# Gate and up tiles of an FFN made by seven products instead of eight

## The chip, the cores and the metric

The kernel runs on one NeuronCore of a Trainium2 chip. The time of a run is its device time in microseconds. A profile describes one execution of the program; its span runs from the first to the last instruction.

Engines are named as in the profile: PE is TensorE's matmuls and PEld its weight loads, DVE is VectorE, ACT is ScalarE, POOL is GpSimd, SP issues most transfers.

## The reference

One inference step of a two-layer decoder trunk. 512 prompt tokens and 8 sample tokens stand side by side as 520 columns of an activation with 1024 features. Each layer is an FFN, a mixer (retention, windowed attention and a convolution over one input projection), and a second FFN:

```
x += 0.5 * (silu(h @ wg) * (h @ wu)) @ wd      h = rmsnorm(x), 1024 -> 2816 -> 1024
x += mix(rmsnorm(x))
x += 0.5 * (silu(h @ wg) * (h @ wu)) @ wd      the second FFN, weights of its own
```

Everything is in 32-bit floating point.

## The kernel before, in words

**Precision.** A 32-bit value is split into a high and a low part: ACT casts it to fp32r (`wh`, `xh`), DVE subtracts (`wl`, `xl`). A product is three matmuls: high by low, high by high, low by high. The activation is transposed, features on partitions and 520 columns along a row, and a matmul covers half of them (260 columns, `HN`). A tile of weights is 128 x 128. `mm3` (L320 to L326) issues the six matmuls of one weight tile; all of its matmuls carry L323.

**Weights.** They come as chunks of 128 x 1024 in the order of use, on SP's queue, into four raw buffers. `split_hi` (ACT, L272) and `split_lo` (DVE, L278) split them ahead of use. A chunk counts two slots, a product's weights (128 x 512) one, and `ahead` keeps everything within six slots of the current unit split.

**An FFN.** It has 22 hidden tiles of 128 features. `hidden` (L391) makes one: eight weight tiles for gate and eight for up, 96 matmuls, into two PSUM tiles. Then DVE multiplies gate by the norm's factor R (L399), ACT takes Silu (L401), DVE multiplies up by R (L402) and both together (L403): u, the hidden tile. Because R is multiplied in afterwards, xh and xl hold x times the norm's gain.

The order is fixed by `ffn_steps`: hidden 0 to 8, down 0, hidden 9 to 16, down 1, hidden 17 to 21, down 2. Down 0 and 1 take eight hidden tiles each in the 2x2 scheme; down 2 takes the last six by plain `mm3`.

**The 2x2 scheme** multiplies a 2 x 2 block matrix of weights by one of activations with seven block products instead of eight, at the price of sums of blocks. Here the blocks of activations are two feature tiles by two halves of the columns. `pair_blocks` (L406) makes them from two hidden tiles: four DVE subtractions (L411 to L414) and their splits (L336, L337). The sums of weights are DVE's too (`sums`, L240 to L245). `pair_down` (L426) runs the products a11, s1, s2, a12, s3, s4, a22 (`PRODUCTS`), each 12 matmuls (L315), and adds four result blocks into x (L433). Partial results are shared by copies on ACT: the first product's c11 is copied into c22 (L436), on which the third product s2 accumulates; two more copies (L439, L442) follow later. Three PSUM tiles of four are in use in one such sequence.

Before an FFN's down step, u of tile 8 (even, first of a pair) is only kept. u of tile 16 is split at once, by the two operations L336 and L337, because the last group isn't paired.

**Order of the engines.** The program is under a manual schedule: each engine runs its instructions in the order in which the Python code issues them.

**Buffers.** `units` is a pool of 20 buffers of 128 x 1040 values for blocks, splits and the mixer's tiles. `cc` holds all constants of the shapes, 2184 columns, loaded once at the start.

Of the kernel before, what the change touches and what calls it, by code (L numbers as in the profile page):

```python
# [10 lines left out]
F32 = mybir.dt.float32  # L11
F32R = mybir.dt.float32r
# [32 lines left out]

C_OFF, C_COLS = {}, 0
for _n, _w in (
    ("ident", 128), ("decT", 512), ("qdec", 256), ("kdec", 4), ("cd", 2), ("gs", 2),
    ("bias", 1024), ("bias32", 128), ("blk64", 128),
):  # L50
    C_OFF[_n] = C_COLS
    C_COLS += _w


def shape_constants():
# [77 lines left out]
def step_kernel(ctx: ExitStack, tc: tile.TileContext, io: dict):  # L133
    nc = tc.nc

    def pool(name, bufs, **kw):
        return ctx.enter_context(tc.tile_pool(name=name, bufs=bufs, **kw))
# [1 line left out]
    const = pool("const", 1)  # L139
    wraw = pool("wraw", RAW)  # L140
    wspl = pool("wspl", 3)
    units = pool("units", 20)
    work = pool("work", 6)
    small = pool("small", 1)
    psum = pool("psum", 4, space=bass.MemoryType.PSUM)
# [7 lines left out]

    Rd = const.tile([128, 2, NT], F32, name="Rd")
    par = const.tile([128, DEPTH, P_COLS], F32, name="par")
    cc = const.tile([128, C_COLS], F32, name="cc")
    epst = const.tile([128, 1], F32, name="epst")
    ones = {}

    def cst(name, *shape):  # L160
        n = int(np.prod(shape))
        a = cc[:, C_OFF[name] : C_OFF[name] + n]
        if len(shape) == 2:
            a = a.rearrange("p (a b) -> p a b", a=shape[0])
        return a
# [38 lines left out]
    for _ in range(DEPTH):  # L204
        for part in range(3):
            if part == 1:
                add_chunks(MIX_CHUNKS)
                continue
            for step, n in ffn_steps():
                if step == "hidden":  # L210
                    add_chunks(2 * KD // CT)
                elif GROUPS[n][2]:
                    add_products(KD // 2)
                else:
                    add_chunks((GROUPS[n][1] - GROUPS[n][0]) * KD // CT)
# [88 lines left out]
    def product(name, o, blocks, first):  # L304

        u, c = at
        assert seq[u][0] == name and c == 0
        ahead(u)
        at[0] = u + 1
        h, lo = spl[u]  # L310
        for j in range(JP):
            s = slice(j * 128, (j + 1) * 128)
            bh, bl = blocks[j][name]
            for i, (a, b) in enumerate(((h, bl), (h, bh), (lo, bh))):
                nc.tensor.matmul(  # L315
                    o, lhsT=a[:, s], rhs=b, start=first and j == 0 and i == 0, stop=j == JP - 1 and i == 2,
                    skip_group_check=True,
                )
# [16 lines left out]
    def split(h, lo, src):  # L335
        nc.scalar.copy(h, src)  # L336
        nc.vector.tensor_sub(lo, src, h.bitcast(F32))  # L337
# [41 lines left out]
    def norm():  # L379
        ah, al = wt("ah", dt=F32R), wt("al", dt=F32R)  # L380
        nc.scalar.copy(ah, acc)
        yield
        nc.vector.tensor_sub(al, acc, ah.bitcast(F32))
        yield
        o = ptile()
        colsum(o, ones[1024], (ah, al))
        yield
        yield from rsqrt(R, o)
        yield
# [13 lines left out]
        nc.vector.tensor_mul(u, u, t)  # L403
        return u

    def pair_blocks(u, w):  # L406


        (b11, b12), (b21, b22) = ((z[:, :HN], z[:, HN:]) for z in (u, w))
        p, q = wt("tp"), wt("tq")  # L410
        nc.vector.tensor_sub(p[:, :HN], b12, b11)  # L411
        nc.vector.tensor_sub(q[:, :HN], b12, b22)
        nc.vector.tensor_sub(p[:, HN:], b11, q[:, :HN])
        nc.vector.tensor_sub(q[:, HN:], b21, p[:, HN:])  # L414
        (bh, th), (bl, tl) = ((unit(F32R), unit(F32R)) for _ in range(2))
        for h, lo, c, n, src in (
            (bh, bl, 0, HN, b11), (bh, bl, HN, NT, w), (th, tl, 0, NT, p), (th, tl, NT, NT, q),
        ):
            split(h[:, c : c + n], lo[:, c : c + n], src[:, :n])
        at = dict(a11=(0, 0), a12=(0, 1), s4=(0, 2), s1=(1, 0), s2=(1, 1), s3=(1, 2), a22=(1, 3))  # L420
        return {
            name: tuple(z[i][:, c * HN : (c + 1) * HN] for z in ((bh, th), (bl, tl)))
            for name, (i, c) in at.items()
        }

    def pair_down(m, blocks):  # L426

        one, mid, c22 = ptile(), ptile(), ptile()[:, 0, :HN]
        c11, c21, m5, c12 = (t[:, i, :HN] for t in (one, mid) for i in range(2))

        def add(half, src, i=0, n=2):
            d = x[:, m + i : m + i + n, half * HN : (half + 1) * HN]
            nc.vector.scalar_tensor_tensor(d, src, 0.5, d, op0=ALU.mult, op1=ALU.add)  # L433

        product("a11", c11, blocks, True)
        nc.scalar.copy(c22, c11)  # L436
# [5 lines left out]
        nc.scalar.copy(c21, c22)  # L442
        product("s4", c12, blocks, False)
        add(1, c22.unsqueeze(1), 1, 1)
        add(1, c12.unsqueeze(1), 0, 1)
        add(1, m5.unsqueeze(1).to_broadcast([128, 2, HN]))
        product("a22", c21, blocks, False)
        add(0, one[:, :, :HN])

    def ffn(norm, after):  # L450
        hs, even = {n: [] for n in range(len(GROUPS))}, None
        for step, n in ffn_steps():
            if step == "hidden":
                g = next(i for i, (a, b, _) in enumerate(GROUPS) if a <= n < b)
                u = hidden(norm, n == 0)
                if not GROUPS[g][2]:
                    h = v2(unit(F32R))
                    hs[g].append((h[:, 0], h[:, 1]))
                    split(*hs[g][-1], u)
                elif n % 2:  # L460
                    hs[g].append(pair_blocks(even, u))
                else:
                    even = u
                continue
            if GROUPS[n][2]:
                for m in range(0, KD, 2):
                    pair_down(m, hs[n])
                continue
            for m in range(KD):
                o = ptile()  # L470
                for f, h in enumerate(hs[n]):
                    mm3(o, next_tile(), *h, f == 0, f == len(hs[n]) - 1)
                nc.vector.scalar_tensor_tensor(
                    v2(x[:, m]), o[:, :, :HN], 0.5, v2(x[:, m]), op0=ALU.mult, op1=ALU.add
                )
                if n == len(GROUPS) - 1:
                    run(after(m))

    def mix(l, after):
# [394 lines left out]
        def ret_vs():  # L874
            o = ptile()
            nc.tensor.transpose(o[:32, 0, :128], vs.rearrange("p h b -> p (h b)"), ident)
            yield
            vst = small.tile([32, 128], F32, tag="vst", name="vst")
            nc.scalar.copy(vst, o[:32, 0, :128])
            sc = ret["sc"] = dram.tile([32, 128], F32, tag="sc", name="sc")  # L880
            nc.gpsimd.dma_start(sc, vst)
            yield
# [279 lines left out]
        yield  # L1162

    for l in range(DEPTH):
        ffn(norm() if l else first_norm, lambda m: prep(l, "mix_norm", m))
        mix(l, lambda m: prep(l, "ffn2_norm", m))
        if l + 1 < DEPTH:
            ffn(norm(), lambda m: prep(l + 1, "ffn1_norm", m))
        else:
            ffn(norm(), store)  # L1170


def host_arrays(i):
# [67 lines left out]
    a["cc"] = shape_constants()  # L1241
# [49 lines left out]
```

## Time and profile before

| | us |
|---|---|
| median of 3 runs | 1939.46 |
| lowest and highest of them | 1937.09, 1940.21 |
| profiled execution | 1931.96 |
| its span | 1930.2 |
| PE, DVE, ACT busy in the span | 1900.1, 1240.2, 789.8 |
| matmuls | 15806 |

The profiled execution's own time is 7.5 us under the median; sums made from its rows are set against its own time. In a row of a timeline the columns are the start, the duration, engine, line, operation, output<-inputs, shapes and count; in square brackets stands how long the engine had been idle and what released it. In a row of groups the columns after the bar are busy time in us and mean ns of one instruction. In a row of windows they are the stretch, its length, the busy time of PE, PEld, DVE, ACT and POOL with instruction counts, the granted TensorE clock (1.00 is full), the DMA share and GB/s.

### The profile page before, as it was taken

Reading aid. Unit: us, or ns where it says so; the run is one execution under the profiler, and the core shown is the slowest. Engines: PE = TensorE matmul, PEld = TensorE weight load, DVE = VectorE, ACT = ScalarE, POOL = GpSimd, SP = SyncE. Lnnn points to the kernel's source line nnn. Section 1 sums busy time; section 2 is a strip of 40 time slices with the busy share of each in tenths; the row PEclk is TensorE's granted clock in tenths of the full one; section 3 lists DMA queues with packets and bytes.
Section 4 is the critical chain, followed back from the end, with each engine's and each line's share of the span. In section 5 each row is a group of like instructions: output and inputs, shape, how many; then the busy total and the mean of one; then the engine's idle time right before and its main releaser. Section 6 shows DMA issues by size and latency. Waiting matters only on the chain.

```text
span 1930.2 us, 36738 instructions
## 1 busy us (share of the span) xinstructions
PE 1900.1 (98%) x15806; PEld 1884.4 (98%) x15806; DVE 1240.2 (64%) x1887; ACT 789.8 (41%) x1280; POOL 21.4 (1%) x48
## 2 busy tenths in 40 slices
PE   8999999999999999999999999999998999999999
PEld 8999999999889999999999999999998999999999
DVE  6585584688757575584555855746887565855843
ACT  5343342433764343343343433425338543433421
POOL 0000000000100000000000000000000000000000
PEclk9999999999999999999999999999999999999999
DMA  5223233333312323323222232323333132232321
GB/s 210 90 77 110 88 99 99 115 107 113 115 45 86 100 70 118 99 70 117 92 95 88 88 110 67 121 97 118 99 112 103 44 99 95 82 110 88 98 100 67
DMA packets 53588, 188.28 MB, mean 98 GB/s; under 512 B 6209, under 2 KB 6961, under 8 KB 53297
## 3 DMA queue, kind: packets, MB, share of 16 engines
q1 hardware_dynamic: 50784, 178.40, 28.2%
q0 software_dynamic: 2496, 7.43, 1.2%
q8 instruction: 124, 2.03, 0.4%
q14 instruction: 40, 0.32, 0.1%
q10 hardware_dynamic: 144, 0.11, 0.0%
HBM read 178.45 MB, written 7.45 MB: 96 GB/s over the span
## 4 chain that ended last, share of the span: by engine, by line
PE 95%; DVE 2%; ACT 2%; issue 0%; DMA 0%; POOL 0%; ACTq 0%; DVEq 0%
PE o L323 76%; PE o L315 16%; PE o L342 1%; DVE nt L360 0%; PE o L1004 0%; PE o L507 0%; PE o L768 0%; PE o L756 0%; DMA m<-sc 0%; PE o L956 0%; DVE rr L361 0%; ACT rsq L1017 0%; ACT m L741 0%; ACT y L357 0%; ACT m L993 0%
## 5 line engine op out<-in xcount | busy, mean ns | idle before, releaser
L323 PE MATMUL o<-xl,wh 128*128 128x260 f32 x3584 | 723.8, 283 | 6.7 <-DVE xl L368 5.8
L323 PE MATMUL o<-xh,wl 128*128 128x260 f32 x3584 | 722.8, 283 | 0.3 <-DVE wl L278 0.3
L323 PE MATMUL o<-xh,wh 128*128 128x260 f32 x3584 | 721.8, 283 | 0.0
L323 PEld LDWEIGHTS o<-xl,wh 128*128 128x128 f32 x3584 | 553.4, 189 | 7.7 <-ACT wh L336 5.8
L323 PEld LDWEIGHTS o<-xh,wl 128*128 128x128 f32 x3584 | 553.3, 189 | 0.5 <-DVE wl L278 0.5
L323 PEld LDWEIGHTS o<-xh,wh 128*128 128x128 f32 x3584 | 551.8, 188 | 0.0
L272 ACT CAST wh<-w 128x1024 fp32r<-128x1024 f32 (+1 forms) x318 | 306.3, 965 | 424.0 <-PE o L323 310.9
L278 DVE TENSOR_TENSOR wl<-w,wh 128x1024 fp32r<-128x1024 f32 x254 | 310.1, 1223 | 222.9 <-ACT wh L272 221.4
L402 DVE TENSOR_TENSOR u<-o,R 128x520 f32<-128x520 f32 x88 | 61.6, 700 | 231.3 <-PE o L323 231.3
L315 PE MATMUL o<-m,wh 128*128 128x260 f32 x1344 | 180.5, 283 | 8.1 <-ACT o L436 8.1
L315 PE MATMUL o<-m,wl 128*128 128x260 f32 x1344 | 179.6, 283 | 0.0
L315 PEld LDWEIGHTS o<-m,wh 128*128 128x128 f32 x1344 | 168.9, 188 | 9.7 <-ACT o L436 9.7
L315 PEld LDWEIGHTS o<-m,wl 128*128 128x128 f32 x1344 | 169.0, 188 | 0.0
L323 PE MATMUL o<-m,wh 128*128 128x260 f32 x1024 | 164.4, 282 | 0.0
L323 PEld LDWEIGHTS o<-m,wh 128*128 128x128 f32 x1024 | 140.3, 188 | 0.0
L336 ACT CAST m<-u 128x260 fp32r<-128x260 f32 (+1 forms) x88 | 47.9, 544 | 196.9 <-DVE u L403 196.9
L401 ACT ACTIVATE t<-t 128x520 f32<-128x520 f32 x88 | 56.4, 641 | 160.9 <-DVE t L399 160.9
L323 PE MATMUL o<-m,wl 128*128 128x260 f32 x512 | 102.8, 282 | 0.0
L585 DVE SCALAR_TENSOR_TENSOR m<-m,par 128x512 f32<-128x512 f32 x120 | 90.1, 750 | 2.9
L433 DVE SCALAR_TENSOR_TENSOR x<-o,x 128x520 f32<-128x520 f32 (+1 forms) x128 | 72.0, 562 | 29.9 <-PE o L315 19.3
L323 PEld LDWEIGHTS o<-m,wl 128*128 128x128 f32 x512 | 78.9, 188 | 0.0
L403 DVE TENSOR_TENSOR u<-u,t 128x520 f32<-128x520 f32 x88 | 61.7, 701 | 9.6 <-DVE u L402 0.5
(193 smaller groups left out, 1363.4 us busy)
## 6 DMA issues: line engine op xcount, KB each, us to landing
w<-in_w SPq DMA_DIRECT2D x318, 512.0 KB, 3.7
out_y<-x SPq DMA_DIRECT2D x8, 260.0 KB, 2.0
m<-in_s_ret SPq DMA_DIRECT2D x4, 512.0 KB, 5.4
m<-sc POOLq DMA_DIRECT2D x8, 256.0 KB, 4.9
out_o_rets<-m POOLq DMA_DIRECT2D x4, 512.0 KB, 3.8
x<-in_x SPq DMA_DIRECT2D x3, 520.0 KB, 6.2
cc<-in_cc SPq DMA_DIRECT2D x1, 1092.0 KB, 10.4
w<-in_w SPq DMA_DIRECT2D x4, 256.0 KB, 4.8
```

The costliest lines, as they stand in the source:

```text
L272: nc.scalar.copy(spl[u][0], source(u))
L278: nc.vector.tensor_sub(lo, source(u), h.bitcast(F32))
L315: nc.tensor.matmul(o, lhsT=a[:, s], rhs=b, start=first and j == 0 and i == 0, stop=j == JP - 1 and i == 2, skip_group_check=True,)
L323: nc.tensor.matmul(o[:, s, :HN], lhsT=a, rhs=b[:, s * HN : (s + 1) * HN], start=first and i == 0, stop=last and i == 2,)
L336: nc.scalar.copy(h, src)
L342: nc.tensor.matmul(o[:, s, :HN], lhsT=w, rhs=v[:, s * HN : (s + 1) * HN], start=i == 0, stop=i == len(parts) - 1,)
L401: nc.scalar.activation(t, t, AF.Silu)
L402: nc.vector.tensor_mul(v2(u), ou[:, :, :HN], v2(R))
L403: nc.vector.tensor_mul(u, u, t)
L433: nc.vector.scalar_tensor_tensor(d, src, 0.5, d, op0=ALU.mult, op1=ALU.add)
L585: nc.vector.scalar_tensor_tensor(y[:, :SEQ], ub[:, j : j + SEQ], w, y[:, :SEQ], op0=ALU.mult, op1=ALU.add)
```

## The change

Fourteen of the 22 hidden tiles (`PAIRED`: 4, 5, 6, 8, 9, 10, 12, 13, 14, 16, 17, 18, 20, 21) are made by `pair_hidden`: gate and up are the two block rows of the weights, pairs of the eight feature tiles of x the block columns, and the two halves of the 520 columns the blocks of the activation. One sequence of seven products with 84 matmuls takes the place of 96.

- `seven` is the body of pair_down, with what differs passed in: `early` after s1 (pair_hidden copies m5 to SBUF on ACT), `late` before a22 (pair_down adds three results; pair_hidden does an add and a multiply by R for each of gate and up, second half), `last` after a22 (pair_hidden multiplies the first halves by R, then Silu and the product).
- `input_sums` makes the blocks of x times gain for two feature tiles: two scaled copies on ACT, four subtractions, two splits. It is called four times in an FFN, behind hidden 0 (once), 1 (twice) and 2 (once), and holds eight units to the end of hidden 21.
- `pair_blocks` now splits b11, b21 and b22 first, then subtracts in place, then splits the four sums. Its three small splits lie in shared units (`spare`). It is called where it was, directly behind the odd tiles 1 to 15.
- u of tile 16 is kept and split after down 1; u of 17 to 21 directly behind its tile, as before.
- `units` has 22 buffers. The constants that only the mixer needs (2048 columns) leave `cc` and are loaded into two units, by two POOL transfers, ahead of each mixer: before down 2 of the first FFN of each layer.
- `vst` takes over the buffer of `p32`. On the host, weights of the fourteen tiles are laid out as a21, a11, a22, a12.

```
+PAIRED = (4, 5, 6, 8, 9, 10, 12, 13, 14, 16, 17, 18, 20, 21)
...
-    units = pool("units", 20)
+    units = pool("units", 22)
...
+    def load_mix_constants():
+        mixc[:] = [unit() for _ in range(2)]
+        for t, a in zip(mixc, io["cm"]):
+            nc.gpsimd.dma_start(t[:, :1024], a)
...
-                if step == "hidden":
+                if step == "hidden" and n in PAIRED:
+                    add_products(1)
+                elif step == "hidden":
                     add_chunks(2 * KD // CT)
...
+    def sums4(u, w):
         (b11, b12), (b21, b22) = ((z[:, :HN], z[:, HN:]) for z in (u, w))
+        nc.vector.tensor_sub(b22, b12, b22)
+        nc.vector.tensor_sub(b12, b12, b11)
+        nc.vector.tensor_sub(b11, b11, b22)
+        nc.vector.tensor_sub(b21, b21, b11)
+        return u, w
...
+    def input_sums(l, name, j):
+        xg = []
+        for k in (2 * j, 2 * j + 1):
+            xg.append(wt("xg"))
+            nc.scalar.activation(xg[-1], x[:, k], AF.Copy, scale=prm(l, name, k))
+        th, tl = unit(F32R), unit(F32R)
+        for i, t in enumerate(sums4(*xg)):
+            c = slice(i * NT, (i + 1) * NT)
+            split(th[:, c], tl[:, c], t)
...
+    def pair_blocks(u, w, spare):
+        if not spare:
+            z = [unit(F32R) for _ in range(3)]
+            spare += [z[i // 4][:, i % 4 * HN : (i % 4 + 1) * HN] for i in range(12)]
+        th, tl = unit(F32R), unit(F32R)
+        b = [(spare.pop(0), spare.pop(0)) for _ in range(3)]
...
+        for d, src in zip(b, (u[:, :HN], w[:, :HN], w[:, HN:])):
+            split(*d, src)
+        for i, src in enumerate(sums4(u, w)):
+            c = slice(i * NT, (i + 1) * NT)
+            split(th[:, c], tl[:, c], src)
...
+    def seven(blocks, late, last, early=None):
         one, mid, c22 = ptile(), ptile(), ptile()[:, 0, :HN]
         c11, c21, m5, c12 = (t[:, i, :HN] for t in (one, mid) for i in range(2))
         product("a11", c11, blocks, True)
         nc.scalar.copy(c22, c11)
         product("s1", m5, blocks, True)
+        if early:
+            early(m5)
         product("s2", c22, blocks, False)
         nc.scalar.copy(c12, c22)
         product("a12", c11, blocks, False)
         product("s3", c22, blocks, False)
         nc.scalar.copy(c21, c22)
         product("s4", c12, blocks, False)
+        late(c12, c22, m5)
         product("a22", c21, blocks, False)
+        last(one)
...
+    def pair_hidden(blocks):
+        t, u, v = wt("t"), wt("u"), wt("v")[:, :HN]
+        def late(c12, c22, m5):
+            for d, c in ((t, c12), (u, c22)):
+                nc.vector.tensor_add(d[:, HN:], c, v)
+                nc.vector.tensor_mul(d[:, HN:], d[:, HN:], R[:, HN:])
+        def last(one):
+            for i, d in enumerate((t, u)):
+                nc.vector.tensor_mul(d[:, :HN], one[:, i, :HN], R[:, :HN])
+            table(SILU)
+            nc.scalar.activation(t, t, AF.Silu)
+            nc.vector.tensor_mul(u, u, t)
+        seven(blocks, late, last, lambda m5: nc.scalar.copy(v, m5))
+        return u
...
+    def ffn(l, name, norm, after):
+        hs, even, spare, xs = {n: [] for n in range(len(GROUPS))}, None, [], []
         for step, n in ffn_steps():
             if step == "hidden":
                 g = next(i for i, (a, b, _) in enumerate(GROUPS) if a <= n < b)
+                u = pair_hidden(xs) if n in PAIRED else hidden(norm, n == 0)
                 if not GROUPS[g][2]:
+                    if n > GROUPS[g][0]:
+                        hs[g].append(two_parts(u))
+                    else:
+                        even = u
                 elif n % 2:
+                    hs[g].append(pair_blocks(even, u, spare))
                 else:
                     even = u
+                xs += [input_sums(l, name, j) for j in ((0,), (1, 2), (3,))[n]] if n < 3 else []
                 continue
             if GROUPS[n][2]:
                 for m in range(0, KD, 2):
                     pair_down(m, hs[n])
+                if not GROUPS[n + 1][2]:
+                    hs[n + 1].append(two_parts(even))
                 continue
+            if n == len(GROUPS) - 1 and name == "ffn1_norm":
+                load_mix_constants()
```

More of the change, by code (lines that the diff above doesn't have):

```diff
@@ L47 @@
 for _n, _w in (
-    ("ident", 128), ("decT", 512), ("qdec", 256), ("kdec", 4), ("cd", 2), ("gs", 2),
-    ("bias", 1024), ("bias32", 128), ("blk64", 128),
+    ("ident", 128), ("kdec", 4), ("cd", 2), ("gs", 2), ("bias", 1024), ("decT", 512), ("qdec", 256), ("bias32", 128),
+    ("blk64", 128),
 ):
@@ L52 @@
     C_COLS += _w
+C_MIX = C_OFF["bias"]
 def shape_constants():
@@ L155, in step_kernel @@
     par = const.tile([128, DEPTH, P_COLS], F32, name="par")
-    cc = const.tile([128, C_COLS], F32, name="cc")
+    cc = const.tile([128, C_MIX], F32, name="cc")
+    mixc = []
     epst = const.tile([128, 1], F32, name="epst")
@@ L161, in cst @@
         n = int(np.prod(shape))
-        a = cc[:, C_OFF[name] : C_OFF[name] + n]
+        c = C_OFF[name]
+        if c < C_MIX:
+            a = cc[:, c : c + n]
+        else:
+            c -= C_MIX
+            a = mixc[c // 1024][:, c % 1024 : c % 1024 + n]
         if len(shape) == 2:
@@ L404, in hidden @@
         return u
-    def pair_blocks(u, w):
+    def sums4(u, w):
         (b11, b12), (b21, b22) = ((z[:, :HN], z[:, HN:]) for z in (u, w))
[L410 to L424, printed above, removed]
@@ L426, in pair_down @@
-    def pair_down(m, blocks):
+        nc.vector.tensor_sub(b22, b12, b22)
[3 more added lines that the diff above has]
+        return u, w
+    MEET = dict(a11=(0, 0), a12=(0, 1), s4=(0, 2), s2=(1, 0), s1=(1, 1), a22=(1, 2), s3=(1, 3))
+    def input_sums(l, name, j):
[7 more added lines that the diff above has]
+            split(th[:, c], tl[:, c], t)
+        e, o = 2 * j, 2 * j + 1
+        b = [tuple(z[:, k, h * HN : (h + 1) * HN] for z in (xh, xl)) for k, h in ((e, 0), (o, 0), (o, 1))]
+        t = [tuple(z[:, i * HN : (i + 1) * HN] for z in (th, tl)) for i in range(4)]
+        return {n: (b, t)[i][c] for n, (i, c) in MEET.items()}
@@ new lines, in pair_blocks @@
+    def pair_blocks(u, w, spare):
[4 more added lines that the diff above has]
+        b = [(spare.pop(0), spare.pop(0)) for _ in range(3)]
+        t = [tuple(z[:, i * HN : (i + 1) * HN] for z in (th, tl)) for i in range(4)]
+        for d, src in zip(b, (u[:, :HN], w[:, :HN], w[:, HN:])):
[3 more added lines that the diff above has]
+            split(th[:, c], tl[:, c], src)
+        return {n: (b, t)[i][c] for n, (i, c) in MEET.items()}
@@ L428, in pair_down @@
+    def seven(blocks, late, last, early=None):
         one, mid, c22 = ptile(), ptile(), ptile()[:, 0, :HN]
         c11, c21, m5, c12 = (t[:, i, :HN] for t in (one, mid) for i in range(2))
-        def add(half, src, i=0, n=2):
-            d = x[:, m + i : m + i + n, half * HN : (half + 1) * HN]
-            nc.vector.scalar_tensor_tensor(d, src, 0.5, d, op0=ALU.mult, op1=ALU.add)
         product("a11", c11, blocks, True)
@@ L443, in pair_down, with add, late, two_parts @@
         product("s4", c12, blocks, False)
-        add(1, c22.unsqueeze(1), 1, 1)
-        add(1, c12.unsqueeze(1), 0, 1)
-        add(1, m5.unsqueeze(1).to_broadcast([128, 2, HN]))
+        late(c12, c22, m5)
         product("a22", c21, blocks, False)
-        add(0, one[:, :, :HN])
-    def ffn(norm, after):
-        hs, even = {n: [] for n in range(len(GROUPS))}, None
+        last(one)
+    def pair_down(m, blocks):
+        def add(half, src, i=0, n=2):
+            d = x[:, m + i : m + i + n, half * HN : (half + 1) * HN]
+            nc.vector.scalar_tensor_tensor(d, src, 0.5, d, op0=ALU.mult, op1=ALU.add)
+        def late(c12, c22, m5):
+            add(1, c22.unsqueeze(1), 1, 1)
+            add(1, c12.unsqueeze(1), 0, 1)
+            add(1, m5.unsqueeze(1).to_broadcast([128, 2, HN]))
+        seven(blocks, late, lambda one: add(0, one[:, :, :HN]))
+    def pair_hidden(blocks):
+        t, u, v = wt("t"), wt("u"), wt("v")[:, :HN]
+        def late(c12, c22, m5):
+            for d, c in ((t, c12), (u, c22)):
[9 more added lines that the diff above has]
+        return u
+    def two_parts(u):
+        h = v2(unit(F32R))
+        split(h[:, 0], h[:, 1], u)
+        return h[:, 0], h[:, 1]
+    def ffn(l, name, norm, after):
+        hs, even, spare, xs = {n: [] for n in range(len(GROUPS))}, None, [], []
         for step, n in ffn_steps():
@@ L454, in ffn @@
                 g = next(i for i, (a, b, _) in enumerate(GROUPS) if a <= n < b)
-                u = hidden(norm, n == 0)
+                u = pair_hidden(xs) if n in PAIRED else hidden(norm, n == 0)
                 if not GROUPS[g][2]:
-                    h = v2(unit(F32R))
-                    hs[g].append((h[:, 0], h[:, 1]))
-                    split(*hs[g][-1], u)
+                    if n > GROUPS[g][0]:
+                        hs[g].append(two_parts(u))
+                    else:
+                        even = u
                 elif n % 2:
-                    hs[g].append(pair_blocks(even, u))
+                    hs[g].append(pair_blocks(even, u, spare))
                 else:
                     even = u
+                xs += [input_sums(l, name, j) for j in ((0,), (1, 2), (3,))[n]] if n < 3 else []
                 continue
@@ L877, in ret_vs @@
             yield
-            vst = small.tile([32, 128], F32, tag="vst", name="vst")
+            vst = small.tile([32, 128], F32, tag="p32", name="vst")
             nc.scalar.copy(vst, o[:32, 0, :128])
@@ L1164, in step_kernel @@
     for l in range(DEPTH):
-        ffn(norm() if l else first_norm, lambda m: prep(l, "mix_norm", m))
+        ffn(l, "ffn1_norm", norm() if l else first_norm, lambda m: prep(l, "mix_norm", m))
         mix(l, lambda m: prep(l, "ffn2_norm", m))
         if l + 1 < DEPTH:
-            ffn(norm(), lambda m: prep(l + 1, "ffn1_norm", m))
+            ffn(l, "ffn2_norm", norm(), lambda m: prep(l + 1, "ffn1_norm", m))
         else:
-            ffn(norm(), store)
+            ffn(l, "ffn2_norm", norm(), store)
 def host_arrays(i):
@@ L1196, in host_arrays @@
             if step == "hidden":
-                chunks.append(t[:, n].reshape(DEPTH, -1, 128, 1024))
+                g = t[:, n]
+                if n in PAIRED:
+                    g = g.reshape(DEPTH, 2, 128, JP, 2, 128)[:, ::-1].transpose(0, 4, 2, 1, 3, 5)
+                chunks.append(g.reshape(DEPTH, -1, 128, 1024))
                 continue
@@ L1240, in host_arrays @@
     a["par"] = np.concatenate([par[n] for n in P_OFF], axis=2)
-    a["cc"] = shape_constants()
+    cc = shape_constants()
+    a["cc"], a["cm"] = cc[:, :C_MIX], cc[:, C_MIX:].reshape(128, 2, 1024).transpose(1, 0, 2)
     s_conv = np.pad(f["state_conv"], ((0, 0), (0, 0), (0, 1), (0, 0)))
```

## The prediction

> **What bounds it.** I read the page first, then the stretches of the first FFN, then who TensorE waits for.
>
> ```profile
> span 1930.2 us, 36738 instructions
> PE 1900.1 (98%) x15806; PEld 1884.4 (98%) x15806; DVE 1240.2 (64%) x1887; ACT 789.8 (41%) x1280; POOL 21.4 (1%) x48
> PE 95%; DVE 2%; ACT 2%; issue 0%; DMA 0%; POOL 0%; ACTq 0%; DVEq 0%
> ```
> ```profile
> 16.00:112.00 96.00, 96.00 (x800) 95.82 (x799) 58.26 (x86) 35.69 (x49) 0.00 (x0) 1.00 0.30 100
> 112.00:153.00 41.00, 40.70 (x339) 40.49 (x339) 33.77 (x57) 21.54 (x40) 0.00 (x0) 1.00 0.35 116
> ```
> ```profile
> PE o L756 <- ACT m L750: 9.3, 2, 4.6
> PE o L315 <- ACT o L436: 8.1, 8, 1.7
> ```
>
> The matmuls are the chain (95%). In plain gate and up tiles (16 to 112 us; the columns after the length are PE, PEld, DVE, ACT busy) TensorE never pauses: 96.00 us over 800 matmuls, 0.12 us each. In seven-product stretches (112 to 153 us, the first pair_down calls) it nearly doesn't, but DVE goes from 61% to 82%. Of TensorE's few waits one concerns the change: the wait on the copy of L436, eight times in the whole run, once per entry into a run of seven-product sequences.
>
> **The gain on TensorE.** A plain tile is 2 x 8 x 6 = 96 matmuls, 11.52 us at 0.12; seven products are 7 x 12 = 84 matmuls of the same 128x128x260 form, 10.08 us. So 1.44 us a tile, 14 tiles, 4 FFNs: 56 x 1.44 = 80.6 us less. Were nothing late, the profiled execution would go from 1931.96 to 1851 us.
>
> **What comes late.** In a seven-product sequence the first product goes to c11, ACT copies c11 into c22, the second product goes elsewhere, and the third (s2) accumulates on the copy. The copy therefore has two products, 2 x 1.44 = 2.88 us, to get done. But on ACT it is issued behind everything written before it: the Silu of the tile before, the casts of that tile's blocks, and the casts of weights taken ahead. Today's entry behind tile 8, behind which no blocks are made:
>
> ```profile
> 112.20 1.60 PE L315 MATMUL o<-m,wh 128*128 128x260 f32 x12
> 113.20 0.70 DVE L403 TENSOR_TENSOR u<-u,t 128x520 f32<-128x520 f32 x1
> 113.64 1.60 PE L315 MATMUL o<-m,wl 128*128 128x260 f32 x12
> 113.82 0.68 DVE L245 TENSOR_TENSOR Rd<-w,Rd 128x512 f32<-128x512 f32 x1
> 114.59 0.62 ACT L272 CAST wl<-Rd 128x512 fp32r<-128x512 f32 x1 [1.22 <-DVE Rd L245]
> 115.12 0.37 ACT L436 COPY o<-o 128x260 f32<-128x260 f32 x1
> 115.54 1.70 PE L315 MATMUL o<-m,wh 128*128 128x260 f32 x12 [0.30 <-ACT o L436]
> ```
>
> u is done at 113.90, only then DVE forms s4's weights (L245), ACT casts them, then copies; s2 starts at 115.54 instead of 112.20 + 2.88 = 115.08: 0.46 us late. The entry behind tile 16 has one split of u (L336, L337) between:
>
> ```profile
> 245.33 1.59 PE L315 MATMUL o<-m,wh 128*128 128x260 f32 x12
> 246.34 0.70 DVE L403 TENSOR_TENSOR u<-u,t 128x520 f32<-128x520 f32 x1
> 247.07 0.63 ACT L336 CAST m<-u 128x520 fp32r<-128x520 f32 x1 [1.08 <-DVE u L403]
> 247.74 0.70 DVE L337 TENSOR_TENSOR m<-u,m 128x520 fp32r<-128x520 f32 x1 [0.70 <-ACT m L336]
> 249.65 0.37 ACT L436 COPY o<-o 128x260 f32<-128x260 f32 x1
> 250.07 1.10 PE L315 MATMUL o<-m,wh 128*128 128x260 f32 x7 [1.73 <-ACT o L436]
> ```
>
> There s2 is due at 248.21 and comes at 250.07: 1.86 us late. Today nothing larger than that split stands ahead of a sequence, because pair_blocks is always followed by a plain tile, which has no copy. After the change every pair_blocks from tile 3 on (3, 5, 7, 9, 11, 13, 15) is directly followed by a seven-product tile. That is 28 sites in four FFNs, and this decides the forecast.
>
> The price of pair_blocks, from u done to DVE's next work, as it is now:
>
> ```profile
> 101.67 0.70 DVE L403 TENSOR_TENSOR u<-u,t 128x520 f32<-128x520 f32 x1
> 102.29 0.42 DVE L411 TENSOR_TENSOR tp<-u 128x260 f32<-128x260 f32 x1
> 106.06 0.69 DVE L240 TENSOR_TENSOR Rd<-w 128x512 f32<-128x512 f32 x1
> ```
>
> 3.77 us of DVE. The new order splits b11, b21, b22 first and then makes the four sums in place, so the casts of b21 and b22 stand between u and the sums; with DVE operations following each other at about 0.34 us (260 wide) and 0.61 (520), and the casts and latencies below, I get 4.28: 0.5 more.
>
> *Plain tile with blocks, then seven products* (3, 7, 11, 15): the chain at 112 us with 4.28 put between L403 and L245: 0.46 + 4.28 = 4.74 us of idle TensorE.
>
> *Seven-product tile with blocks, then seven products* (5, 9, 13): here u itself is later. What DVE does between the end of s4 and the last operation of a sequence is in pair_down today:
>
> ```profile
> 121.40 1.60 PE L315 MATMUL o<-m,wh 128*128 128x260 f32 x12
> 121.60 1.16 DVE L433 SCALAR_TENSOR_TENSOR x<-o,x 128x260 f32<-128x260 f32 x2 [0.50 <-PE o L315]
> 122.68 0.68 DVE L278 TENSOR_TENSOR wh<-w,wh 128x512 fp32r<-128x512 f32 x1
> 123.28 0.68 DVE L245 TENSOR_TENSOR Rd<-w,Rd 128x512 f32<-128x512 f32 x1
> 123.88 0.69 DVE L433 SCALAR_TENSOR_TENSOR x<-o,x 128x520 f32<-128x520 f32 x1
> ```
>
> 121.40 is where a22 starts, so it ends at 122.84; the last operation starts at 123.88, behind a weight split and a weight sum of 0.6 each. In pair_hidden the late part is four 260-wide operations, add and multiply twice, each multiply depending on its add (0.46 + 0.34, twice: 1.6 us). So the final multiplies start 0.2 + 1.6 + 1.2 = 3.0 us after a22 starts, 1.56 after it ends. Then the first of them (0.43), Silu, the product with it (0.70):
>
> ```profile
> L401 ACT ACTIVATE t<-t 128x520 f32<-128x520 f32 x88 | 56.4, 641 | 160.9 <-DVE t L399 160.9
> L433 DVE SCALAR_TENSOR_TENSOR x<-o,x 128x260 f32<-128x260 f32 x64 | 27.4, 428 | 28.8 <-PE o L315 19.3 <-ACT o L442 9.5
> L336 ACT CAST m<-u 128x260 fp32r<-128x260 f32 x32 | 12.6, 394 | 0.0
> L366 ACT ACTIVATE xh<-x,par 128x520 fp32r<-128x520 f32 x48 | 35.0, 731 | 69.4 <-DVE x L473 51.0 <-DVE x L1061 16.5 <-DMA par<-in_par 1.7
> ```
>
> u is ready 1.56 + 0.43 + 0.05 + 0.64 + 0.05 + 0.70 = 3.4 us after a22. From u, ACT's last cast of blocks ends 3.5 later (casts of b21 and b22 0.7, their subtractions and three sums to 2.3, two 520-wide casts 1.2); then one weight cast (0.5) and the copy (0.4): s2 starts 7.8 us after a22's end, due at 2.88: 4.9 us idle.
>
> *The smaller sites, in each FFN.* Seven products behind a seven-product tile with nothing between (4 to 5, 12 to 13, 8 and 16 into pair_down): Silu ends 2.7 after a22, weight cast and copy take it to 3.55: 0.67 x 4 = 2.7. With two_parts between (17, 20): its cast waits for u, 4.94 - 2.88 = 2.06, twice, 4.1. Plain tile 19 with two_parts: as measured at 245 us, 1.86. Tile 21 into the last down: its halves are ready 4.9 after a22, and needed after five of six tiles, 30 x 0.12 = 3.6: 1.3. The input sums: behind tile 1 stand pair_blocks and two input_sums, each two scaled copies (0.73, the L366 row), four 260-wide sums, two casts, two subtractions, some 3.7 us of waiting chain; with the 1.7 us until u and the next chunk's split this is about 14.7 us, against the 11.52 + 0.48 that tile 2 covers: 2.7 late at tile 3. The same behind tiles 0 and 2 fits in the tile's cover.
>
> Sum per FFN: 4 x 4.74 + 3 x 4.89 + 2.7 + 4.1 + 1.86 + 1.3 + 2.7 = 46.3; less the 0.46 + 1.86 of today: 44.0. Four FFNs: 176 us. Bounds of the 28 sites: from 3.77 (today's pair_blocks alone, the latency before it free) to 5.4 (half a microsecond of other DVE work in front), so 106 to 151 us against the 135 of the sum.
>
> **The clock behind the waits.** Idle stretches of this length stand twice in the run, in the mix:
>
> ```profile
> 527.51 1.14 PE L729 MATMUL o<-m 64*128 64x256 f32 x8
> 533.29 1.97 PE L756 MATMUL o<-cc,m 128*128 128x128 f32 x8 [4.64 <-ACT m L750]
> ```
> ```profile
> 532.00:534.00 2.00, 0.71 (x4) 0.60 (x4) 1.97 (x3) 2.00 (x6) 0.00 (x0) 0.53 0.01 4
> 534.00:536.00 2.00, 2.00 (x10) 1.42 (x10) 1.97 (x4) 1.94 (x5) 0.00 (x0) 0.50 0.00 0
> 536.00:538.00 2.00, 2.00 (x12) 1.64 (x11) 1.97 (x4) 2.00 (x9) 0.00 (x0) 0.50 0.00 0
> 538.00:540.00 2.00, 2.00 (x14) 1.20 (x14) 1.93 (x4) 2.00 (x7) 0.00 (x0) 0.76 0.00 0
> ```
> ```profile
> core 0: 1930.2 us, clock 0.996
> ```
>
> After 3.4 us of idleness the granted clock (third column from the right) falls to half and stays there until about 538.9; TensorE works 5.6 us of that, so 2.8 us are lost beside the wait. The mean of 0.996 leaves 7.7 us over the run, room for the two stretches of L756 at 3.4 each and little else: both were hit, and the waits of up to 1.73 us at L436 were not. Sites of 4.7 to 4.9 us are as long as these; I bound the loss by none (0) and all (28 x 2.8 = 78 us) and take 6 in 10, because two of two speak for all, but a drop that comes after 3.4 of 4.8 us has room to miss: 47 us.
>
> [...]
>
> **Edits at nothing.** The mix's constants are two POOL transfers of 512 KB per mix, issued ahead of the last down, which runs some 35 us (288 matmuls); POOL is busy 21.4 us in the run and has nothing queued behind that an engine awaits there. Uncovered, a transfer like those on POOL lands in about 5 us: 0 to 10 us. The smaller constant load at the start precedes nothing that TensorE awaits; 0. Two more units and the shared p32 tile add no wait I can find; 0. The weights are the same bytes, in the order that pair_down already reads.
>
> **The sum.** 1931.96 - 80.6 + 176 + 47 = 2074 us for a profiled execution. The median shown, 1939.46, is 7.5 above the profiled one; so 2082 us.
>
> **Rivals.** *The waits without the clock*: as above with no site hit: 2035 us. For it: the drop came only after 3.4 us; against: the sites are longer than the stretch that dropped. *Every site hit*: 2113 us. *Faster, DVE sets the pace*: the copies come in time because ACT has caught up, and the rest is DVE's load. Four pair_down sequences take DVE 33.77 us, 8.4 each; pair_hidden has seven closing operations (six of 0.43, one of 0.70) for pair_down's 2.26 us and an idle 0.5 for Silu, about 10 each. Three of those, a plain tile of 5.1 (58.26 us over 8.3 tiles, less 3.77 for each second) and two pair_blocks of 4.2 make 43.5 us of DVE, against TensorE's 3 x 10.08 + 11.52 = 41.8 and 46.1 before: 2.6 gained in four tiles, 56/3 times: 48 us, 1891 us. It decides if the mean wait at the 28 sites stays under (80.6 - 41) / 28 = 1.4 us, where 41 us are the smaller sites' net; with all waits, 2.9 us is what would eat the whole 80.6. Against it: the 245 us entry already waits 1.73 us for one split. *The copy isn't held up at all*: 1939.46 - 80.6 = 1859 us; it needs ACT to run the copy ahead of casts written before it, and both entries above show it behind them. *No difference*: the sites average about 1.4 us and gain and loss cancel; nothing speaks for just that.
>
> **Chances.** The forecast 0.50, no clock loss 0.23, every site hit 0.15, faster by DVE's pace or by no wait 0.10, no difference 0.02. Slower 0.88, same 0.02, faster 0.10; 0.2% (4 us) is about what a measurement of this kernel tells from no change. The likeliest case's own range is 2045 to 2110; with the bounds of the sites (-29 to +16) and of the clock (-47 to +31) it reaches from 2006 to 2129, which I round outward to 1995 and 2130.
>
> **What would show it.** TensorE's instructions fall by 672, to 15134. Its waits on the copy into c22 rise from 8.1 us to over 130, in some 50 places, with 28 of 4 to 5 us at tiles 4, 6, 8, 10, 12, 14, 16 of each FFN; plain tiles stay near 11.5 us; the granted clock shows half-speed stretches behind a part of these. ACT before the copy shows the casts of blocks, each waiting for DVE's sums. Wrong would be: waits below 1.4 us there, or DVE busy above 95% through tiles 4 to 16, with a time below the old one.

## The result and the profile after

The changed kernel takes 2120.24 us (median of four runs, 2114.48 to 2124.24), the kernel before 1938.28 (1933.60 to 1940.21): a ratio of 1.094, 95% interval 1.0906 to 1.0975. It is slower by 9.4%, inside the stated range, and nearest to the rival in which the clock drops at every site (2113). Why that rival came so near is in part chance, as the account of the clock below shows.

The page's first lines and TensorE's waits (in total, times, longest), after:

```profile
span 2120.4 us, 37000 instructions
PE 1907.9 (90%) x15134; PEld 1879.3 (89%) x15134; DVE 1606.4 (76%) x2743; ACT 1004.0 (47%) x1880; POOL 23.3 (1%) x52
```
```profile
PE o L333 <- ACT o L472: 170.4, 56, 5.6
PE o L341 <- ACT wh L290: 15.3, 4, 3.9
PE o L834 <- ACT m L828: 9.2, 2, 4.6
PE o L341 <- DVE m L355: 4.1, 4, 1.0
```
```profile
core 0: 2120.4 us, clock 0.951
```

L472 is now the copy of c11 into c22 (L436 before). The span grew by 190.2 us, and these rows split it. TensorE is not busy for 2120.4 - 1907.9 = 212.5 us, before 30.1: 182.4 us more. It is busy 7.8 us longer although it has 672 matmuls less; these are worth 80.6 us at full clock, so its work takes 88.4 us longer than at full clock. Nearly all of that is the clock: by the record of the granted clock in the two traces, TensorE is busy for 177.9 us at half clock after and for 10.8 us before, and half of the difference, 83.5 us, is lost. The 5 us left over were not followed up. The mean clock fell from 0.996 to 0.951.

A site behind a plain tile (3 into 4), in the timeline; the product s1 ends about where the DVE sums begin:

```profile
62.28 0.70 DVE L421 TENSOR_TENSOR u<-u,t 128x520 f32<-128x520 f32 x1
63.02 0.72 ACT L354 CAST m<-u 128x260 fp32r<-128x260 f32 x2 [0.47 <-DVE u L421]
64.26 0.43 DVE L428 TENSOR_TENSOR u<-u 128x260 f32<-128x260 f32 x1
64.73 0.43 DVE L429 TENSOR_TENSOR u<-u 128x260 f32<-128x260 f32 x1
65.19 0.43 DVE L430 TENSOR_TENSOR u<-u 128x260 f32<-128x260 f32 x1
65.66 1.15 ACT L354 CAST m<-u 128x520 fp32r<-128x520 f32 x2 [1.92 <-DVE u L430]
66.31 1.31 DVE L355 TENSOR_TENSOR m<-u,m 128x520 fp32r<-128x520 f32 x2 [0.23 <-ACT m L354]
66.72 0.61 ACT L290 CAST wh<-w 128x512 fp32r<-128x512 f32 x1
67.54 0.68 DVE L263 TENSOR_TENSOR Rd<-w,Rd 128x512 f32<-128x512 f32 x1
68.32 0.62 ACT L290 CAST wl<-Rd 128x512 fp32r<-128x512 f32 x1 [0.99 <-DVE Rd L263]
68.84 0.37 ACT L472 COPY o<-o 128x260 f32<-128x260 f32 x1
69.26 2.97 PE L333 MATMUL o<-m,wh 128*128 128x260 f32 x12 [5.04 <-ACT o L472]
```

Between u (62.98) and s2 (69.26) stand, on ACT and DVE in turn, the blocks' casts, sums and subtractions, the sum for s4, two weight casts, and only then the copy. The first product there takes 2.97 us; at full clock such a row shows 1.60, as the first one below does. A site behind a seven-product tile (5 into 6):

```profile
90.25 1.60 PE L333 MATMUL o<-m,wl 128*128 128x260 f32 x12
91.51 0.70 DVE L511 TENSOR_TENSOR u<-u,t 128x520 f32<-128x520 f32 x1 [0.37 <-ACT t L510]
94.87 1.15 ACT L354 CAST m<-u 128x520 fp32r<-128x520 f32 x2 [1.91 <-DVE u L430]
95.93 0.61 ACT L290 CAST wl<-Rd 128x512 fp32r<-128x512 f32 x1
96.45 0.37 ACT L472 COPY o<-o 128x260 f32<-128x260 f32 x1
96.87 2.97 PE L333 MATMUL o<-m,wh 128*128 128x260 f32 x12 [5.02 <-ACT o L472]
```

The windows around the first site (third column from the right is the granted clock) show the half-speed stretch that begins as TensorE starts again:

```profile
64.00:69.00 5.00, 0.23 (x2) 0.02 (x1) 4.50 (x10) 2.35 (x5) 0.00 (x0) 1.00 0.00 0
69.00:71.00 2.00, 1.74 (x8) 1.74 (x9) 1.87 (x4) 1.54 (x4) 0.00 (x0) 0.53 0.59 147
71.00:73.00 2.00, 2.00 (x13) 2.00 (x13) 1.97 (x4) 0.68 (x2) 0.00 (x0) 0.62 0.80 219
73.00:75.00 2.00, 2.00 (x19) 2.00 (x18) 1.14 (x3) 0.85 (x2) 0.00 (x0) 1.00 0.39 158
```

### The profile page after: what moved, and what is told of

Same layout as the page of the kernel before. It is cut to its first block, busy times and chain, and to the rows that moved or that the text cites. A ratio compares the mean times of both kernels' runs of the same rounds, so it can differ in the third digit from the quotient of the medians.

```text
span 2120.4 us, 37000 instructions
## 1 busy us (share of the span) xinstructions
PE 1907.9 (90%) x15134; PEld 1879.3 (89%) x15134; DVE 1606.4 (76%) x2743; ACT 1004.0 (47%) x1880; POOL 23.3 (1%) x52
## 5 line engine op out<-in xcount | busy, mean ns | idle before, releaser
L333 PE MATMUL o<-m,wh 128*128 128x260 f32 x2688 | 381.8, 294 | 92.0 <-ACT o L472 92.0
L333 PEld LDWEIGHTS o<-m,wh 128*128 128x128 f32 x2688 | 356.2, 198 | 97.8 <-ACT o L472 97.8
L341 PE MATMUL o<-xl,wh 128*128 128x260 f32 x1792 | 367.0, 286 | 21.7 <-ACT wh L290 15.3
L341 PE MATMUL o<-xh,wl 128*128 128x260 f32 x1792 | 364.8, 285 | 1.6 <-DVE wl L296 1.4
L341 PE MATMUL o<-xh,wh 128*128 128x260 f32 x1792 | 363.5, 285 | 0.0
L290 ACT CAST wh<-w 128x512 fp32r<-128x512 f32 (+1 forms) x318 | 256.7, 810 | 169.8 <-PE o L341 100.5
L341 PEld LDWEIGHTS o<-xl,wh 128*128 128x128 f32 x1792 | 280.2, 191 | 23.7 <-ACT wh L290 16.1
L341 PEld LDWEIGHTS o<-xh,wl 128*128 128x128 f32 x1792 | 279.5, 191 | 2.8 <-DVE wl L296 2.8
L341 PEld LDWEIGHTS o<-xh,wh 128*128 128x128 f32 x1792 | 279.1, 190 | 0.0
L296 DVE TENSOR_TENSOR wl<-w,wh 128x1024 fp32r<-128x1024 f32 x142 | 172.8, 1222 | 74.6 <-ACT wh L290 73.0
L341 PE MATMUL o<-m,wh 128*128 128x260 f32 x1024 | 164.5, 282 | 4.1 <-DVE m L355 4.1
L333 PE MATMUL o<-xh,wh 128*128 128x260 f32 x672 | 144.7, 313 | 0.0
L341 PEld LDWEIGHTS o<-m,wh 128*128 128x128 f32 x1024 | 140.0, 188 | 4.9 <-DVE m L355 4.9
L290 ACT CAST wh<-Rd 128x512 fp32r<-128x512 f32 x132 | 81.7, 619 | 107.4 <-DVE Rd L261 54.8
L290 ACT CAST wl<-Rd 128x512 fp32r<-128x512 f32 x132 | 81.8, 619 | 102.9 <-DVE Rd L261 52.0
L333 PE MATMUL o<-xh,wl 128*128 128x260 f32 x672 | 128.5, 289 | 0.0
L333 PEld LDWEIGHTS o<-xh,wh 128*128 128x128 f32 x672 | 122.1, 221 | 0.0
L296 DVE TENSOR_TENSOR wh<-w,wh 128x512 fp32r<-128x512 f32 x176 | 120.5, 684 | 1.6
L296 DVE TENSOR_TENSOR wl<-w,wl 128x512 fp32r<-128x512 f32 x176 | 120.4, 684 | 1.1
```

The lines of the kernel that those rows point to most:

```text
L290: nc.scalar.copy(spl[u][0], source(u))
L296: nc.vector.tensor_sub(lo, source(u), h.bitcast(F32))
L333: nc.tensor.matmul(o, lhsT=a[:, s], rhs=b, start=first and j == 0 and i == 0, stop=j == JP - 1 and i == 2, skip_group_check=True,)
L341: nc.tensor.matmul(o[:, s, :HN], lhsT=a, rhs=b[:, s * HN : (s + 1) * HN], start=first and i == 0, stop=last and i == 2,)
```

## The experiments

The kernel before was run beside each group; its medians there were 1934.28 (first four), 1934.29 (next four) and 1933.59 (last). Ratios are to it.

**Everything but the pairing.**

```
-PAIRED = (4, 5, 6, 8, 9, 10, 12, 13, 14, 16, 17, 18, 20, 21)
+PAIRED = ()
-                xs += [input_sums(...) ...] if n < 3 else []
+                xs += [input_sums(...) ...] if PAIRED and n < 3 else []
```

> All of the change but the seven-product hidden tiles: no tile is paired and no input sums are made, while the mix's constants are loaded anew, pair_blocks has its new order and tile 16 is split behind down 1. Theory (the loss is the place of pair_blocks ahead of a copy, and the clock behind it): within 4 us of the kernel before, about 1935, since the wait ahead of down 1 shrinks from 1.86 to 0.46 us in four FFNs (-6 us); TensorE's waits fall to about 17 us. Rival (the constants, the two more units or the new pair_blocks cost something themselves): 1945 or more, with a wait on the two new transfers or on units.

1932.09 us, ratio 0.9985 (0.9974 to 0.9995).

```profile
PE o L333 <- ACT o L472: 6.9, 8, 0.9
```

The time is as expected, but the 6 us of waits did not fall away: these were 8.1 us before. Ahead of down 1, where tile 16's split caused 1.7, they are 0.83 to 0.89; ahead of down 0 they rose from 0.3 to about the same, and what raised them was not followed up. In the time, the mix's constants, the units and the new form of pair_blocks cost nothing that can be seen; the loss is in the pairing.

**Ten tiles, pair_blocks never ahead of a sequence.**

```
+PAIRED = (5, 7, 9, 11, 13, 15, 17, 18, 20, 21)
```

> Ten tiles made by seven products in place of fourteen, chosen so that every pair_blocks from tile 3 on is followed by a plain tile: 5, 7, 9, 11, 13, 15, 17, 18, 20, 21. Theory: the 28 waits of 5 us on the copy are gone and their share of the slow clock too; 40 x 1.44 = 57.6 us of matmuls less, against small waits of about 12 us per FFN (seven of 0.5, two of 1.9, one of 1.7, one of 1.0, the input sums 3.9, less today's 2.3) and some 18 us of slow clock: about 1945 us. Rival (a seven-product hidden tile is slow in itself, by DVE's load): the excess goes by the number of such tiles, 40/56 of 182, so about 2068 us.

1997.14 us, ratio 1.0319 (1.0293 to 1.0345): between the two expectations. The waits of 5 us are gone, as the theory said, but the small entries are not 0.5 us:

```profile
PE o L333 <- ACT o L472: 55.6, 40, 1.9
PE o L333 <- DVE t L417: 18.9, 24, 0.9
```
```profile
96.51 0.68 DVE L296 TENSOR_TENSOR wh<-w,wh 128x512 fp32r<-128x512 f32 x1
97.11 0.69 DVE L417 TENSOR_TENSOR t<-o,R 128x520 f32<-128x520 f32 x1
99.13 0.68 DVE L263 TENSOR_TENSOR Rd<-w,Rd 128x512 f32<-128x512 f32 x1
```
```profile
99.90 0.62 ACT L290 CAST wh<-Rd 128x512 fp32r<-128x512 f32 x1 [0.92 <-DVE Rd L263]
100.43 0.37 ACT L472 COPY o<-o 128x260 f32<-128x260 f32 x1
```

DVE comes late to the plain tile's gate (L417), behind pair_blocks, four weight splits and two weight sums. s1 waits for the PSUM tile that L417 reads (0.8 us), then s2 for the copy behind a weight cast that waits for L263 (1.2 us). I had priced these entries with a DVE that was free.

**TensorE kept busy in the pauses.**

```
         if early:
             early(m5)
+        if fill[0]:
+            idle = ptile()
+            for i in range(fill[0]):
+                nc.tensor.matmul(idle[:, i % 2, :HN], lhsT=xh[:, 0, :128], rhs=xh[:, 1, :HN], start=True, stop=True)
+            fill[0] = 0
...
+                fill[0] = 40 if n in (4, 6, 8, 10, 12, 14, 16) else 0
```

> The changed kernel with 40 matmuls (4.8 us at full clock) into an unused PSUM tile between s1 and s2 of tiles 4, 6, 8, 10, 12, 14 and 16, where TensorE stands idle; their result is read by nobody. Theory (the clock falls because TensorE is idle, and costs about 88 us beside the waits): s2 starts as late as before, but the half-speed stretches behind these 28 sites go; 2040 to 2060 us, mean clock above 0.98. Rival (the clock has little to do with the time, the waits are all of it): 2120 us or more, since 28 x 40 matmuls are added.

2064.57 us, ratio 1.0671 (1.0652 to 1.0689), some 56 us less than the changed kernel by the medians, with 1120 matmuls more.

```profile
core 0: 2063.3 us, clock 0.986
```
```profile
PE o L333 <- ACT o L474: 33.7, 45, 2.0
```

The mean clock is back at 0.986, as expected; the time is 5 us above the range I gave. In the trace no half-speed stretch is left at the 28 sites, and the loss at half clock is 25.7 us in place of 88.9, of which these sites had 61. So the clock is a cost of its own, caused by idleness, and 56 us of it show in the time. 130 us over the kernel before remain, while TensorE computes nothing of use in these waits.

**The same fourteen tiles, pair_blocks moved into the sequence that follows.** Its splits of b11, b21 and b22, its sums, and the splits of the sums become three steps of a generator:

```
         nc.scalar.copy(c22, c11)
+        next_side()
...
         nc.scalar.copy(c12, c22)
+        next_side()
...
         nc.scalar.copy(c21, c22)
+        next_side()
```

> The changed kernel with the same fourteen tiles; the work of pair_blocks moved into the sequence that follows, in three parts, behind the copies into c22, c12 and c21. Theory: the copy into c22 no longer has blocks ahead of it and its wait falls from 5.0 to below 1 us where DVE is not behind; but DVE has 14.4 us of work in a sequence of 10.1, so part of the wait returns on late operations of DVE: 1930 to 1990 us, DVE busy over 85%. Rival (what precedes the copy on ACT is not the cause): waits on the copy stay near 170 us and the time near 2120.

2015.31 us, ratio 1.0416 (1.0386 to 1.0445). By moving alone 105 us come back; the range I gave ended at 1990, and DVE is busy for 79% of the span (1593.3 of 2020.4 us) where I expected over 85%. The waits of 5 us are gone, and shorter ones stand in their place, behind DVE:

```profile
PE o L333 <- ACT o L486: 56.4, 56, 1.9
PE o L333 <- ACT o L496: 40.3, 16, 2.5
```
```profile
72.13 0.62 ACT L290 CAST wl<-Rd 128x512 fp32r<-128x512 f32 x1 [3.09 <-DVE Rd L261]
72.66 0.37 ACT L496 COPY o<-o 128x260 f32<-128x260 f32 x1
73.08 1.72 PE L333 MATMUL o<-m,wh 128*128 128x260 f32 x12 [2.52 <-ACT o L496]
```

The copy into c21 (L496) now waits behind a cast of summed weights, which DVE made late because it was at the blocks' sums.

**Nine tiles and a better order.** The next two take what the ten-tile run showed, one part each. In the first, the product a11 no longer takes later weights ahead (its last argument); that is done behind the copy.

```
+PAIRED = (5, 7, 9, 11, 13, 15, 17, 19, 21)
...
-        product("a11", c11, blocks, True)
+        product("a11", c11, blocks, True, False)
         nc.scalar.copy(c22, c11)
+        ahead(at[0] - 1)
+        if side:
+            side.append(two_parts(side.pop()))
...
-                xs += [input_sums(l, name, j) for j in ((0,), (1, 2), (3,))[n]] if n < 3 else []
+                xs += [input_sums(l, name, j) for j in ((0,), (), (1, 2), (3,))[n]] if n < 4 else []
```

> Nine tiles by seven products (5, 7, 9, 11, 13, 15, 17, 19, 21), no two in a row. In a sequence the copy into c22 is issued ahead of the casts of later weights, the split of tiles 18 and 20 behind that copy, and the input sums behind tiles 0, 2 (two) and 3. Theory (in the ten-tile run the second part of each wait, 1.24 us, is the copy behind weight casts; the first part, 0.8 us, is s1 waiting for a PSUM tile whose gate half DVE reads late): the 1.24 us parts, the 1.87 us waits and the 3.8 us waits at tile 3 go, the 0.8 us parts stay: 36 x 1.44 = 51.8 us less, 15 to 25 us of waits more than before: 1895 to 1912 us. Rival (DVE's load alone sets these waits, not the order): 1940 us or more.

1922.77 us, ratio 0.9934 (0.9915 to 0.9953): faster than the kernel before by 0.7%, not by as much as expected. Of the waits that the pairing brought, one kind is left:

```profile
PE o L334 <- DVE t L418: 32.4, 28, 3.4
```

Twenty-four of them are the 0.8 us forecast. Four, of 3.4 us, stand in tile 5 of each FFN: there DVE comes to tile 4's gate behind the input sums that now follow tile 3 and the weights' sums and splits after them (in the first FFN the input sums end at 65.44 us and the gate's product starts at 70.76). So the wait of the input sums moved rather than went.

The second part moves the gate's product (L399 before, L418 here) between the halves of a plain tile:

```
+        for i, (o, k) in enumerate(ffn_tiles(first, og, ou)):
+            if i == KD and not first:
+                nc.vector.tensor_mul(v2(t), og[:, :, :HN], v2(R))
             mm3(o, next_tile(), xh[:, k], xl[:, k], k == 0, k == KD - 1)
```

> As the run before, and in a plain tile DVE multiplies the gate by R between the tile's two halves, ahead of the splits of later weights. Theory: the PSUM tile is free in time and the 0.8 us waits of s1 go too; TensorE's waits fall to about the 25 to 35 us of the kernel before; 1880 to 1895 us. Rival (DVE now stops in the middle of the tile and is late afterwards): no faster than the run before.

1911.45 us, ratio 0.9875 (0.9854 to 0.9896). The wait on the gate is gone from the list of TensorE's waits, and 11 us with it; the mechanism holds. The time is 16 us above the range: waits on copies remain, 10.4 us at L485, 6.4 at L477 and 3.3 at L488.

```profile
PE o L334 <- ACT o L485: 10.4, 28, 0.7
PE o L334 <- ACT o L477: 6.4, 4, 1.6
PE o L334 <- ACT o L488: 3.3, 8, 0.4
```

A tenth tile:

```
-PAIRED = (5, 7, 9, 11, 13, 15, 17, 19, 21)
+PAIRED = (5, 7, 9, 11, 13, 15, 17, 18, 20, 21)
```

> As the run before, with 17, 18, 20 and 21 in place of 17, 19 and 21: a tenth tile per FFN, and two pairs of sequences in a row with only a split of u between. Theory: 5.8 us of matmuls less, and 0.2 to 1 us of wait at 18 and 21 (DVE about 11.4 us in a sequence of 10.1): 0 to 6 us faster than nine tiles. Rival (two in a row put DVE behind): slower than nine tiles by 5 us or more.

1909.78 us, ratio 0.9869 (0.9850 to 0.9889). No difference from nine tiles can be told; the two intervals overlap almost wholly.

All fourteen tiles with every one of these means, and with pair_blocks in the following sequence:

> All fourteen tiles, the three parts of pair_blocks in the sequence that follows, the split of u behind the copy, the copy ahead of weight casts, the gate early, input sums behind tiles 0, 1 and 2 (two). Theory (what remains is DVE's amount of work, 43 to 45 us per four tiles against TensorE's 41.8): 1890 to 1960 us, DVE busy 82% or more and the waits on operations behind DVE; not faster than nine or ten tiles. Rival (order alone was the loss): the whole 80 us come in, about 1860 us.

1963.37 us, ratio 1.0141 (1.0120 to 1.0162), just above the range, slower than nine or ten tiles and than the kernel before. DVE is busy 81% of the span (1589.5 of 1963.3 us), and TensorE waits behind it:

```profile
PE o L334 <- ACT o L500: 44.7, 20, 2.9
PE o L334 <- ACT o L489: 19.1, 19, 1.6
```
```profile
117.83 0.62 ACT L290 CAST wh<-Rd 128x512 fp32r<-128x512 f32 x1 [3.09 <-DVE Rd L261]
```

The copy of L500 (c21) follows this cast, which waits for a weight sum that DVE makes behind the four sums of blocks. The order tried here was not the whole loss. That DVE's work in the sequence behind a pair does not fit in any order is argued, not shown: making the weights' sum ahead of the blocks' sums was not tried.

Last, ten tiles with the input sums one tile earlier:

```
-                xs += [input_sums(l, name, j) for j in ((0,), (), (1, 2), (3,))[n]] if n < 4 else []
+                xs += [input_sums(l, name, j) for j in ((0,), (1,), (2, 3))[n]] if n < 3 else []
```

> The ten-tile version with the input sums behind tiles 0, 1 and 2 (two) in place of 0, 2 (two) and 3. Theory (the 1.6 us wait in tile 5 is DVE late by the sums that stand behind tile 3 with pair_blocks): four waits of 1.6 us go and nothing comes at tile 3, since tile 2 has no pair_blocks; 3 to 8 us less than the ten-tile version, about 1904. Rival (DVE is as late from tile 2's two sums): the wait moves to tile 3 or 4 and the time stays.

1908.14 us, ratio 0.9864 (0.9842 to 0.9886). The four waits of 1.6 us are gone from the trace, but no gain over the ten tiles before can be told; waits on a weight split (L296) went from 2.1 to 4.1 us, and in the profiled execution two more stretches at half clock in the mixer raised that loss from 5.6 to 9.8 us (mean clock 0.996 and 0.994). This version and the two with the gate early and nine or ten tiles are about 1.3% faster than the kernel before.

## Why the prediction was right, point by point

**The gain on TensorE** was as counted: 15806 - 15134 = 672 matmuls.

**The sites.** There are 28, in the places named. The trace has 28 pauses of 4.93 to 5.55 us, together 140.8, against 135 in the sum and 106 to 151 as its bounds. Behind plain tiles I had 4.74; twelve of the sixteen show 4.93 to 4.95, and those into tile 4 show 5.00 to 5.55, over my upper bound of 5.4 in two places, for a reason that stays open. The four sums in place start 0.47 us apart (64.26, 64.73 and 65.19 in the rows above, the fourth at 65.66), where I had taken 0.34; that is 0.39 us more in three steps, and the rest of the chain was a little shorter than I had it. Behind seven-product tiles 4.9 was forecast and 5.02 is in the row. What the two edits of the place show (ten tiles, and the moved blocks): without pair_blocks ahead of the copy no wait of this size is left.

**The smaller sites.** The sixteen entries with nothing between two sequences are 0.46 to 0.49 us in place of 0.67; the entries behind two_parts 1.87 and 1.69 (once 2.04) in place of 2.06 and 1.86; down 2 waits 1.0 in place of 1.3. The input sums cost 3.8 us at tile 3, in place of 2.7 (15.3 us in the row of L290). In all TensorE stands 182.4 us longer, forecast 176.

**The clock** is the term of the sum that was mis-sized: 47 us forecast with 6 hits in 10, 83.5 measured. The step that failed is the sentence that a drop which comes after 3.4 of 4.8 us has room to miss. Of the 48 us by which the profiled execution (2122.21) passed the 2074 of the sum, 6 are waits and nearly all of the rest is TensorE's longer work, 88.4 in place of 47. No site missed: the half-speed stretches at the 28 sites began 2.3 to 5.0 us after their pauses did. The kernel before had already shown that 3.4 us is no fixed delay. In its first long pause, from 528.65, the 0.53 in the window from 532 puts the drop at 532.12, 3.47 us in. The second lasts from 1488.32 to 1492.96, and the 0.63 in the window from 1491 puts the drop at 1491.26, 2.9 us into the pause:

```profile
1492.96 1.97 PE L756 MATMUL o<-cc,m 128*128 128x128 f32 x8 [4.64 <-ACT m L750]
```
```profile
1490.00:1491.00 1.00, 0.00 (x0) 0.00 (x0) 0.87 (x2) 0.97 (x3) 0.00 (x0) 1.00 0.00 0
1491.00:1492.00 1.00, 0.00 (x0) 0.00 (x0) 0.96 (x2) 0.97 (x3) 0.00 (x0) 0.63 0.00 0
```

Two more parts of the term were off, in opposite directions. A hit cost 2.2 us on average and not 2.8, because 12 of the 28 stretches lasted 3.41 us and 16 lasted 6.83: together 61 us. And twelve shorter pauses that I had left out were hit too, eight of 1.87 us behind tiles 17 and 20 and four of 3.8 us at tile 3: 20 us more. So the 78 us of the rival with every site hit came near the total by luck. The experiment with TensorE kept busy shows that idleness is the cause: the mean clock was 0.986 there, against 0.951.

**The edits at nothing** were at nothing in the time (0.9985 without the pairing).

**The rivals.** That DVE sets the pace was rejected for this kernel as it stands. Once the copies are moved first, late operations of DVE are what TensorE's largest waits go back to, but fourteen tiles then give 1963 us and not the 1891 of that rival. There I had added up DVE's busy time over four tiles and let it spread evenly; in the trace of that run DVE's work falls together in the sequence behind a pair. How its 29 us over the kernel before divide into DVE's amount of work and DVE's order was not measured.

## What to carry to other kernels

When a product on TensorE depends on a copy by another engine, count what is issued ahead of that copy on its engine, and follow what that work waits for; here a saving of 80.6 us met 28 copies, each behind a chain that went back and forth between ACT and DVE. A saving of matmuls by sums was paid here on the engine that makes the sums (DVE busy 1606.4 us in place of 1240.2): nine or ten tiles with the copy first and the gate early gained 1.3%, fourteen lost 1.4%. A pause of TensorE can cost more than its length, so price the clock behind it too: behind the 28 pauses of 140.8 us here, 61 us more were lost at half clock.

## What the runs showed of the hardware

The clock fell behind shorter pauses than expected. Behind tile 17 (pause of 1.87 us until 344.38):

```profile
344.38 2.00 PE L333 MATMUL o<-m,wl 128*128 128x260 f32 x12 [1.87 <-ACT o L472]
```
```profile
343.00:345.60 2.60, 1.22 (x10) 1.22 (x11) 2.04 (x4) 2.15 (x5) 0.00 (x0) 1.00 0.00 0
345.60:349.00 3.40, 3.40 (x19) 3.40 (x17) 1.65 (x2) 1.32 (x2) 0.00 (x0) 0.50 0.89 243
349.00:352.00 3.00, 3.00 (x26) 3.00 (x26) 0.09 (x2) 1.36 (x3) 0.00 (x0) 1.00 0.71 235
```

TensorE is already at work again for 1.2 us when the clock halves, for 3.4 us: 19 matmuls instead of the 28 that 0.12 us each would give. Counted in the traces of the kernels before and after, leaving out the wait before a program's first matmul, a half-speed stretch began during a pause or within 1.6 us of its end in these numbers: 0 of 8 pauses from 0.88 to 1.18 us, 0 of 7 from 1.69 to 1.73, 8 of 9 from 1.86 to 2.04, 36 of 36 from 3.76 to 5.55. No pause over 0.88 us had another length.

The two traces also show where in time the stretches stand. In the changed kernel the 43 that begin within the span do so whole multiples of 3.413 us apart (at 48.63, 69.11 and 96.42, for example: 6 and 8 times), and each lasts 3.41 or 6.83 us. Cut both traces at such marks, without the first 20 us and the end, and look at the pieces at full clock. Where TensorE idled for 5 to 53.1% of a piece, the next was at half clock in 0 of 73 cases; from 54.4% on in 44 of 44, and no piece lies between. The eight pauses of 1.86 to 1.88 us that were hit fell into one piece each, all but 0.01 us of them, and made up 54.4 to 55.0% of it; of the 2.04 us pause, which was not hit, no piece held more than 44.4%. From these counts, a pause of over 3.7 us (twice 54.4% of 3.413) would be hit wherever it falls; that is an estimate, and all 36 pauses from 3.76 us agree with it, the 28 of 4.93 us and more among them. One drop came without idle time, at 1598.28 in the changed kernel, in the mixer behind a piece with 20 matmuls of two columns (L1082); behind three other pieces with 16, 16 and 12 of them none came. Why is open.

Four DVE operations in place on one another (260 wide, 0.43 us long) started 0.47 us apart, against 0.34 for the two independent ones at 102.29 and 102.63 us of the trace before. That trace showed the larger step too: the two that follow there, each on the result of the one ahead of it, start at 103.08 and 103.55, 0.45 and 0.47 us later.
